# Splitting a query tile: two casts in a row and one subtraction on 128 rows

## The chip, the cores and the metric

One core of a Trainium2 chip runs the kernel. The metric is the device time of one execution in microseconds (us). TensorE (PE; its weight loads are PEld) multiplies, VectorE (DVE), ScalarE (ACT) and GpSimd (POOL) work on tiles, and SyncE (SP) issues nearly all transfers. Each engine runs its own queue in order and waits on semaphores.

## The reference

One decoder layer on x of 2048 x 1024 in float32. Cut to what matters here:

```python
h = rmsnorm(x, norm1)
q, k, v, b_gate, c_gate, hc, p = split(h @ w_in)          # 512 | 128 | 128 | 3 x 256 | 256
scores = einsum('bnqhgd,bnkhd->bnhgqk', qb, k_band) / 8    # 8 query heads of 64, 2 key heads
probs  = softmax over a band of 128 keys, with bias and a sink per head
mixed  = concat([probs @ v_band, short_conv(...), pool(...)])
x = x + mixed @ w_out
x = x + relu(rmsnorm(x, norm2) @ w1)**2 @ w2
out = rmsnorm(x, final_norm)
```

## The kernel before, in words

Matrix products run in TensorE's fp32r format. To keep float32 accuracy each operand is split in two: a high part (ScalarE casts the value to fp32r) and a low part (value minus high part, by VectorE or GpSimd). A product is then three matmuls, high x high, high x low and low x high (lines 285 to 287).

The first part of the kernel, some 620 us, runs over four blocks b of 512 tokens. Channels lie on the 128 rows of a tile, tokens on its columns. In each block 14 column tiles of the input projection are computed in the order `IN_ORDER` (tiles 0 to 3 are queries, 4 keys, 5 values, the others the convolution's and the pool's), each into one of three PSUM banks (`pj`). Eight units of attention, one for each of 128 query rows and each key head, are laid between these projections; then come eight tiles of the output projection (`po`). Block 0 has one peculiarity: its normalisation is applied after the product, so that VectorE writes the product times `rb` to a tile `z` in SBUF, and what follows reads `z`. In blocks 1 to 3 what follows reads the PSUM bank itself. In block 3 VectorE and SP also prepare the MLP's first inputs (`xb`, lines 784 to 830).

For scores, a query tile holds two heads, 64 rows each. `do_q` writes a tile `q` of 128 x 2 x 512: for head a, the high part lies on the head's own 64 rows and the low part on the other 64, so that one matmul against keys stacked in the same way (`Kd`) adds both. The low part is computed on the head's own rows (`ql`), and a transfer on SP carries it to the other 64 rows. The scores (`sc`, lines 610 and 611) of the first unit with these heads need both the cast and the landed transfer.

Weights come through a ring of six raw tiles (`wr`, line 208, on SP's queue), are cast by ScalarE (`wh`, line 263) and completed by GpSimd or VectorE (`wl`, line 264), in a second ring of six.

The order of instructions on each engine is not the order of the code: a scheduler that runs when the program is built places them by estimated times. A change in one function therefore moves instructions elsewhere too. Stores are collected in a list `late` and issued at the next weight step.

Of the kernel before, what the change touches and what calls it, by code (L numbers as in the profile page):

```python
# [12 lines left out]
F32R = mybir.dt.float32r  # L13
I32 = mybir.dt.int32
AF = mybir.ActivationFunctionType
ALU = mybir.AluOpType
# [10 lines left out]
HD = 64  # L27
# [52 lines left out]
def f32(ap):  # L80
    return ap.bitcast(F32)
# [3 lines left out]
def tile_trunk(  # L85
# [14 lines left out]
    pe, act, dve, gp, sp = nc.tensor, nc.scalar, nc.vector, nc.gpsimd, nc.sync  # L100
# [11 lines left out]
    raw_src, plan, late = [], [], []  # L112
# [199 lines left out]
    def tmp(name):  # L312
        return pB.tile([P, T], F32, tag="tmp", name=name, bufs=4)
# [218 lines left out]
    def proj(b, i, mid=None, bank=None):  # L532
        if b == 0 and i in first:
            ps = first[i]
            flush()
        else:
            xh, xl = xhl[b]
            ps = ps_mm.tile([P, T], F32, tag="mm", name=f"pj{b}_{i}") if bank is None else bank
            for k in range(KC):
                if k % HC == 0:  # L540
                    hi, lo = w_next()
                if k == HC and mid:
                    mid()
                latest[0] = mm3(ps, hi[:, k % HC], lo[:, k % HC], xh[:, k], xl[:, k], k == 0, k == KC - 1)
        return ps
# [42 lines left out]
    def do_q(b, i, ps):  # L588
        q = pA.tile([P, 2, T], F32R, tag=f"q{i}", name=f"q{b}_{i}")
        ql = tmp(f"ql{b}_{i}")  # L590
        for a in range(2):
            o = a * 64
            act.copy(q[o : o + 64, a], ps[o : o + 64])
            dve.tensor_tensor(
                out=ql[o : o + 64].bitcast(F32R), in0=ps[o : o + 64], in1=f32(q[o : o + 64, a]), op=ALU.subtract
            )
            z = 64 - o
            late.append(lambda o=o, z=z, a=a: sp.dma_start(f32(q[z : z + 64, a]), ql[o : o + 64]))
        Q[b, i] = q


# [252 lines left out]
    for i in range(4):  # L854
        evac[i] = lambda b, ps, i=i: do_q(b, i, ps)
# [6 lines left out]
    for b in range(NB):  # L862
# [10 lines left out]
        for i in IN_ORDER[:NPRE]:  # L873
            ps = proj(b, i)
# [6 lines left out]
        for n, i in enumerate(IN_ORDER[NPRE:]):  # L881
# [7 lines left out]
            ps = proj(b, i, mid)  # L889
# [329 lines left out]
    kept, ps = {}, {}  # L1219
    for i, (o, q, pp_, cs) in enumerate(steps):  # L1220
# [18 lines left out]
        if q == NQ - 1:  # L1239
# [3 lines left out]
            ps = {}  # L1243
# [98 lines left out]
```

## Time and profile before

| | |
|---|---|
| median of 3 runs | 1916.68 us (1915.47 to 1917.81) |
| the profiled execution | 1912.7 us, span 1910.9 us, mean granted clock 0.992 |
| PE busy | 1875.3 us (98%) |
| DVE, ACT, POOL busy | 1114.4, 894.2, 1020.9 us |
| attention and projections, four blocks | about the first 620 us |

A view by stretches gives busy time of each engine in a window, counted in us from the span's start. A view of waits names the waiting engine and line and what released it. Where a row says `[0.36 <-DMA q<-ql]`, the engine had been idle for 0.36 us and the transfer of ql to q ended that. Line numbers are those of the kernel before; in the changed kernel the lines after 598 have numbers smaller by one.

### The profile page before, as it was taken

To read this page: it belongs to the slowest core of one execution; us is meant where nothing else is said; L and a number is where in the kernel's file an instruction comes from. 1 tells how busy PE (TensorE), PEld (TensorE's weight loads), DVE (VectorE), ACT (ScalarE), POOL (GpSimd) and SP (SyncE) were. 2 spreads that over 40 slices of the span, in tenths; PEclk is the share of its full clock that TensorE was granted. 3 is DMA by queue.
4 is the path that set the end of the run, shared out by engine and by line. 5 is a ranking of instruction groups with operands and counts; after the bars stand their busy time and mean duration, and the time that the engine had idled before them with its cause. 6 is when DMAs were issued, how large, how long until landed. Compare 5 with 4: busy or idle time off the path is not lost.

```text
span 1910.9 us, 25904 instructions
## 1 busy us (share of the span) xinstructions
PE 1875.3 (98%) x8507; PEld 1527.7 (80%) x8507; DVE 1114.4 (58%) x1606; ACT 894.2 (47%) x1637; POOL 1020.9 (53%) x745
## 2 busy tenths in 40 slices
PE   8989999999899999999999999999999999999998
PEld 6867887888787888888878888888888888888887
DVE  5695585576888577865574444442525264533465
ACT  6654664663476444554565455442323222225332
POOL 5667566575563645654464444434666665526520
PEclk9999999999999999999999999999999999999999
DMA  8417426425936779765686656588777666645244
GB/s 261 139 61 219 123 67 208 129 72 183 313 105 217 241 252 316 274 219 195 226 282 202 198 178 194 187 276 281 238 236 237 196 214 203 221 131 166 99 160 138
DMA packets 202938, 375.46 MB, mean 196 GB/s; under 512 B 22775, under 2 KB 43316, under 8 KB 202804
## 3 DMA queue, kind: packets, MB, share of 16 engines
q1 hardware_dynamic: 201992, 373.20, 60.3%
q8 instruction: 67, 1.10, 0.2%
q10 hardware_dynamic: 812, 0.61, 0.1%
q14 instruction: 67, 0.55, 0.1%
HBM read 249.45 MB, written 117.98 MB: 192 GB/s over the span
## 4 chain that ended last, share of the span: by engine, by line
PE 84%; DMA 6%; DVE 6%; issue 2%; ACT 1%; POOL 1%; SPq 1%; DVEq 0%; POOLq 0%; ACTq 0%
PE o L285 11%; PE o L286 11%; PE o L287 11%; PE bT L287 6%; PE bT L286 6%; PE bT L285 6%; PE bB L285 4%; PE bB L286 4%; PE bB L287 4%; PE pj L286 4%; PE pj L285 4%; PE pj L287 4%; PE po L286 1%; PE po L285 1%; PE po L287 1%
## 5 line engine op out<-in xcount | busy, mean ns | idle before, releaser
L264 POOL TENSOR_TENSOR wl<-wr,wh 128x512 fp32r<-128x512 f32 x354 | 502.9, 1427 | 516.0 <-ACT wh L263 477.8
L263 ACT CAST wh<-wr 128x512 fp32r<-128x512 f32 x416 | 254.5, 617 | 345.5 <-PE bT L286 62.6
L784 DVE TENSOR_TENSOR bl<-br,bh 128x1024 fp32r<-128x1024 f32 (+2 forms) x144 | 186.9, 1301 | 320.9 <-ACT bh L1131 318.0
L286 PE MATMUL o<-bl,wh 128*128 128x512 f32 (+1 forms) x960 | 362.0, 380 | 0.0
L287 PE MATMUL o<-bh,wl 128*128 128x512 f32 (+1 forms) x960 | 361.2, 380 | 0.0
L285 PE MATMUL o<-bh,wh 128*128 128x512 f32 (+1 forms) x960 | 349.7, 380 | 0.0
L286 PEld LDWEIGHTS o<-bl,wh 128*128 128x128 f32 x960 | 180.9, 188 | 36.6 <-DVE bl L784 0.2
L287 PEld LDWEIGHTS o<-bh,wl 128*128 128x128 f32 x960 | 180.8, 188 | 36.7
L285 PEld LDWEIGHTS o<-bh,wh 128*128 128x128 f32 x960 | 176.4, 188 | 36.4
L286 PE MATMUL bT<-hlT,wh 128*128 128x512 f32 x512 | 202.2, 395 | 1.0 <-POOL hlT L987 1.0
L287 PE MATMUL bT<-hhT,wl 128*128 128x512 f32 x512 | 202.0, 395 | 0.0
L285 PE MATMUL bT<-hhT,wh 128*128 128x512 f32 x512 | 201.8, 394 | 0.0
L285 PE MATMUL pj<-xh,wh 128*128 128x512 f32 x440 | 177.7, 405 | 7.0 <-ACT wh L263 6.5
L286 PE MATMUL pj<-xl,wh 128*128 128x512 f32 x440 | 176.2, 401 | 4.1 <-DVE xl L419 4.1
L287 PE MATMUL pj<-xh,wl 128*128 128x512 f32 x440 | 176.3, 401 | 0.0
L264 POOL TENSOR_TENSOR wl<-s,wh 128x512 fp32r<-128x512 f32 x64 | 92.2, 1440 | 137.7 <-ACT wh L263 128.9
L263 ACT CAST wh<-s 128x512 fp32r<-128x512 f32 x64 | 39.7, 621 | 247.4 <-PE o L286 238.8
L1131 ACT CAST bh<-br 128x1024 fp32r<-128x1024 f32 (+2 forms) x144 | 123.2, 856 | 64.4 <-PE o L287 55.5
L285 PE MATMUL bB<-hhB,wh 128*128 128x512 f32 x384 | 151.7, 395 | 0.0
L286 PE MATMUL bB<-hlB,wh 128*128 128x512 f32 x384 | 151.4, 394 | 0.0
L287 PE MATMUL bB<-hhB,wl 128*128 128x512 f32 x384 | 151.3, 394 | 0.0
L231 POOL TENSOR_TENSOR s<-wr,wr 128x512 f32<-128x512 f32 x64 | 127.9, 1999 | 15.3 <-DMA wr<-in_w_dram 10.6
(186 smaller groups left out, 3368.5 us busy)
## 6 DMA issues: line engine op xcount, KB each, us to landing
wr<-in_w_dram SPq DMA_DIRECT2D x256, 256.0 KB, 3.6
hop_T<-s SPq DMA_DIRECT2D x128, 256.0 KB, 2.9
wr<-in_win_dram SPq DMA_DIRECT2D x112, 256.0 KB, 4.3
hop_B<-h SPq DMA_DIRECT2D x96, 256.0 KB, 3.3
br<-hop_B SPq DMA_DIRECT2D x48, 512.0 KB, 4.5
br<-hop_T SPq DMA_DIRECT2D x48, 512.0 KB, 4.5
wr<-ss_T SPq DMA_DIRECT2D x48, 256.0 KB, 2.9
wr<-in_wout_dram SPq DMA_DIRECT2D x36, 256.0 KB, 2.6
```

The source lines that it names most:

```text
L231: gp.tensor_tensor(out=t, in0=a, in1=b, op=op)
L263: act.copy(hi, src)
L264: eng.tensor_tensor(out=lo, in0=src, in1=f32(hi), op=ALU.subtract)
L285: pe.matmul(ps, hi, xh, start=first, stop=False)
L286: pe.matmul(ps, hi, xl, start=False, stop=False)
L287: return pe.matmul(ps, lo, xh, start=False, stop=last)
L784: return dve.tensor_tensor(out=out, in0=a, in1=b, op=ALU.subtract)
L1131: mark["act"] = act.copy(hi, src)
```

## The change

ScalarE first casts all 128 rows into the first half of `q` (the rows of head 1 there are scratch, and the transfer of head 0's low part overwrites them), and then the 64 rows of head 1 into the second half. VectorE then subtracts once, on 128 rows. The two transfers are as before, 64 rows each, and both now follow the one subtraction.

```diff
     def do_q(b, i, ps):
         q = pA.tile([P, 2, T], F32R, tag=f"q{i}", name=f"q{b}_{i}")
         ql = tmp(f"ql{b}_{i}")
+
+        act.copy(q[:, 0], ps)
+        act.copy(q[HD:, 1], ps[HD:])
+        dve.tensor_tensor(out=ql.bitcast(F32R), in0=ps, in1=f32(q[:, 0]), op=ALU.subtract)
         for a in range(2):
-            o = a * 64
-            act.copy(q[o : o + 64, a], ps[o : o + 64])
-            dve.tensor_tensor(
-                out=ql[o : o + 64].bitcast(F32R), in0=ps[o : o + 64], in1=f32(q[o : o + 64, a]), op=ALU.subtract
-            )
-            z = 64 - o
-            late.append(lambda o=o, z=z, a=a: sp.dma_start(f32(q[z : z + 64, a]), ql[o : o + 64]))
+            o, z = a * HD, (1 - a) * HD
+            late.append(lambda o=o, z=z, a=a: sp.dma_start(f32(q[z : z + HD, a]), ql[o : o + HD]))
         Q[b, i] = q
```

What the scheduler makes of it is shown at three places. On SP's queue in block 0, where the first query tiles are sent (q_0 and q_1 are the query tiles, ql their low parts, wr a weight load, xr the next block's input, wx a table of weights), before:

```order
L598 DMA q_0_684<-ql_0_685 64x512 x2
L598 DMA q_1_694<-ql_1_695 64x512
L208 DMA wr_782<-in_win_dram 128x512
L377 DMA xr_6_1229<-in_xT_dram 128x512
L598 DMA q_1_694<-ql_1_695 64x512
```

and now:

```order
L597 DMA q_0_684<-ql_0_685 64x512 x2
L208 DMA wr_780<-in_win_dram 128x512
L597 DMA q_1_693<-ql_1_694 64x512 x2
L377 DMA xr_6_1225<-in_xT_dram 128x512
L377 DMA xr_7_1313<-in_xT_dram 128x512
```

q_1's first transfer moved behind a weight load, its second ahead of an input load.

On VectorE in block 3, between the first unit's scores and the second's (s and nm are a unit's scores and their maximum, rd the reciprocal of the denominator, xb the MLP's inputs), before:

```order
L627 RECIPROCAL rd_0_0_5298<-den_0_0_5297 128x4
L784 TENSOR_TENSOR xb_2_5617<-xb_2_5617,xb_3_5618 128x512
L784 TENSOR_TENSOR xb_1_5833<-xb_3_5835,xb_1_5833 128x512
L594 TENSOR_TENSOR ql_3_5471<-pj_3_5404,q_3_5470 64x512
L628 TENSOR_TENSOR s_0_0_5294<-s_0_0_5294,rd_0_0_5298 128x4x256
L594 TENSOR_TENSOR ql_3_5471<-pj_3_5404,q_3_5470 64x512
L620 ISA s_1_0_5385,nm_1_0_5387<-sc_1_0_5376,bias,nsink 128x256
```

and now:

```order
L626 RECIPROCAL rd_0_0_5284<-den_0_0_5283 128x4
L783 TENSOR_TENSOR xb_2_5601<-xb_2_5601,xb_3_5602 128x512
L783 TENSOR_TENSOR xb_1_5817<-xb_3_5819,xb_1_5817 128x512
L627 TENSOR_TENSOR s_0_0_5280<-s_0_0_5280,rd_0_0_5284 128x4x256
L594 TENSOR_TENSOR ql_3_5456<-pj_3_5389,q_3_5455 128x512
L619 ISA s_1_0_5370,nm_1_0_5372<-sc_1_0_5361,bias,nsink 128x256
```

One subtraction is gone and the other stands behind the normalisation of s.

On TensorE in block 0, where the scores of the second unit (1,0) stand among the projection's matmuls (pj_12 and pj_13 are column tiles 12 and 13), before:

```order
L287 MATMUL pj_12_922<-xh_362,wl_761 128x512
L285 MATMUL pj_13_1026<-xh_362,wh_778 128x512
L286 MATMUL pj_13_1026<-xl_363,wh_778 128x512
L287 MATMUL pj_13_1026<-xh_362,wl_779 128x512
L285 MATMUL pj_13_1026<-xh_362,wh_778 128x512
L610 MATMUL sc_1_0_804<-Kd,q_0_684 128x256
```

and now:

```order
L285 MATMUL pj_12_918<-xh_362,wh_758 128x512
L286 MATMUL pj_12_918<-xl_363,wh_758 128x512
L287 MATMUL pj_12_918<-xh_362,wl_759 128x512
L285 MATMUL pj_12_918<-xh_362,wh_758 128x512
L286 MATMUL pj_12_918<-xl_363,wh_758 128x512
L609 MATMUL sc_1_0_801<-Kd,q_0_684 128x256
```

The scores moved ahead of the last matmul of tile 12 and of the first four of tile 13.

## The prediction

> **What bounds the kernel now.** I read the page's head and chain first, then a table by stretches, then TensorE's waits, then the tile that the change touches.
>
> ```profile
> span 1910.9 us, 25904 instructions
> PE 1875.3 (98%) x8507; PEld 1527.7 (80%) x8507; DVE 1114.4 (58%) x1606; ACT 894.2 (47%) x1637; POOL 1020.9 (53%) x745
> ...
> PE 84%; DMA 6%; DVE 6%; issue 2%; ACT 1%; POOL 1%; SPq 1%; DVEq 0%; POOLq 0%; ACTq 0%
> ```
>
> TensorE works 1875.3 of 1910.9 us and makes up 84% of the chain that ended last. Its idle time is 35.6 us in all, and no change to casts and subtractions can win more than a part of that and of what low clocks add to it. So I ask where TensorE is idle while the touched blocks run. In the table by stretches the first number is the stretch's length; then PE, PEld, DVE, ACT and POOL busy time, granted clock, DMA share and GB/s:
>
> ```profile
> 115.00:180.00 65.00, 59.66 (x250) 46.91 (x249) 47.09 (x68) 31.71 (x61) 37.70 (x29) 0.95 0.47 144
> 180.00:250.00 70.00, 69.21 (x351) 57.34 (x350) 42.23 (x106) 45.76 (x110) 44.95 (x40) 1.00 0.48 133
> 500.00:580.00 80.00, 76.66 (x392) 63.20 (x391) 69.14 (x146) 50.70 (x127) 47.44 (x39) 1.00 0.53 176
> 620.00:1200.00 580.00, 579.02 (x2486) 469.01 (x2485) 353.98 (x455) 296.95 (x503) 298.29 (x208) 1.00 0.68 231
> ...
> 60.00:95.00 35.00, 35.00 (x189) 29.76 (x188) 23.50 (x63) 24.47 (x68) 26.76 (x26) 1.00 0.31 87
> 95.00:130.00 35.00, 32.45 (x153) 25.75 (x152) 34.21 (x62) 21.34 (x51) 25.36 (x22) 0.95 0.22 68
> ...
> 135.00:140.00 5.00, 3.91 (x10) 2.86 (x11) 4.44 (x7) 3.72 (x7) 2.31 (x2) 0.70 0.00 0
> ```
>
> Block 1's attention (180 to 250) leaves 0.8 us idle. The end of block 0 (115 to 180) leaves 5.3 us and block 3's attention (500 to 580) 3.3 us; there VectorE is the busy one (34.2 of 35 us from 95 to 130, 69.1 of 80 from 500 to 580). From 620 to 1200 TensorE idles 1.0 us of 580, at 579.02/2486 = 0.233 us per matmul, so time won earlier is kept. After a stall the granted clock is lower for some microseconds (0.70 from 135 to 140), so a stall costs more than its idle time. TensorE's waits by cause (total, times, longest):
>
> ```profile
> PE sc L610 <- DMA q<-ql: 3.4, 5, 1.5
> PE po L285 <- ACT mxh L688: 2.3, 1, 2.3
> PE av L649 <- DVE ao L658: 1.8, 2, 1.7
> PE pt L638 <- DVE s L628: 0.9, 1, 0.9
> PE sc L610 <- DVE nm L620: 0.8, 1, 0.8
> PE po L286 <- POOL mxl L689: 0.7, 1, 0.7
> PE av L650 <- DVE ptl L642: 0.6, 1, 0.6
> ```
>
> Only the first row, 3.4 us, is a wait for a q tile itself, and it is for the transfer, not for the split.
>
> **The change part by part.** What an instruction costs stands in the rows of the tiles (minimum, median, maximum in ns) and in the groups by form:
>
> ```profile
> L593 ACT CAST q<-pj x24: 575/581/584, 189.9 to 528.2; 64x512 fp32r<-64x512 f32 x24
> L594 DVE TENSOR_TENSOR ql<-pj,q x24: 672/688/695, 190.5 to 529.4; 64x512 fp32r<-64x512 f32 x24
> L594 DVE TENSOR_TENSOR ql<-z,q x8: 672/687/1369, 44.3 to 60.7; 64x512 fp32r<-64x512 f32 x8
> ...
> L642 DVE TENSOR_TENSOR ptl<-pt,pth x62: 673/689/693, 67.9 to 589.0; 128x512 fp32r<-128x512 f32 x62
> ...
> L641 ACT CAST pth<-pt 128x512 fp32r<-128x512 f32 x62 | 34.7, 587 | 4.0 <-PE pt L638 3.2
> ```
>
> A 128-row subtraction from PSUM takes 689 ns where a 64-row one takes 688, and a 128-row cast 587 where a 64-row one takes 581. So VectorE goes from 32 subtractions to 16, 16 x 0.688 = 11.0 us less work, and ScalarE keeps 32 casts, 16 of them 128 rows, 0.1 us more. Neither engine sets the span; 11.0 us is an upper bound that only a VectorE-bound stretch could pass on.
>
> The order of waits changes too. Before, in blocks 1 to 3, the second cast waits for the first subtraction and the second subtraction for the second cast (total, times, longest):
>
> ```profile
> ACT q L593 <- DVE ql L594: 14.0, 10, 4.9
> DVE ql L594 <- ACT q L593: 9.1, 9, 2.5
> ```
>
> After, the two casts stand next to each other on ScalarE. I take it that the subtraction follows both, since before no two engines read one PSUM tile at once, not even its two halves (the waits just shown). The 14.0 us of ScalarE's queue held up by VectorE go. ScalarE is idle half the time and no wait of TensorE's above ends on it through these casts, so I price that at nothing: the cover is the ring of six split weight tiles.
>
> *Block 0 (43 to 60 us).* The tile comes from SBUF, so the subtraction needs the first cast only. On SP's queue the first transfer of q_1 now stands behind a weight load:
>
> ```profile
> 46.88 3.66 SPq L598 DMA_DIRECT2D q<-ql  x3
> 50.64 0.53 SPq L208 DMA_DIRECT2D wr<-in_win_dram  x1
> ...
> 52.68 0.48 SPq L598 DMA_DIRECT2D q<-ql  x1
> ...
> 55.32 0.33 PE L610 MATMUL sc<-Kd,q 128*128 128x128 f32 x1 [0.96 <-DMA q<-ql]
> ...
> 56.06 0.33 PE L610 MATMUL sc<-Kd,q 128*128 128x128 f32 x1 [0.30 <-DMA q<-ql]
> ```
>
> The third issue of the first row is q_1's head 0; it gets 0.53 plus about 0.1 us later. Head 1 (52.68) leaves about 1.0 us sooner. q_0's issues, for which TensorE waits 0.96 us at 55.32, follow the wx store as before and do not move. The low end is that block 0's waits go (this one and 0.30 at 56.06, together 1.3 us), the high end that q_1's head 0 adds 0.65 and its transfer as much again behind the load's: +1.2. I take +0.5, since q_1's scores come right behind q_0's.
>
> *Blocks 1 and 2.* The chain for q_1 of block 1, with what TensorE waits for:
>
> ```profile
> 195.45 0.58 ACT L593 CAST q<-pj 64x512 fp32r<-64x512 f32 x1
> 196.07 0.68 DVE L594 TENSOR_TENSOR ql<-pj,q 64x512 fp32r<-64x512 f32 x1
> 196.78 0.58 ACT L593 CAST q<-pj 64x512 fp32r<-64x512 f32 x1 [0.75 <-DVE ql L594]
> 197.45 0.69 DVE L594 TENSOR_TENSOR ql<-pj,q 64x512 fp32r<-64x512 f32 x1
> 196.78 0.47 SPq L598 DMA_DIRECT2D q<-ql  x1
> 198.25 0.47 SPq L598 DMA_DIRECT2D q<-ql  x1
> 203.01 0.36 PE L610 MATMUL sc<-Kd,q 128*128 128x256 f32 x1 [0.36 <-DMA q<-ql]
> ```
>
> Now: 195.45 + 0.58 + 0.58 + about 0.1 of handover + 0.69 = 197.4 for both heads, against 196.75 for head 0 and 198.1 for head 1. Head 0 is 0.65 us late, head 1 is issued 0.5 behind it at about 198.0, 0.2 us early. The wait of 0.36 us is for head 0, so it can grow. The bounds for both blocks are -0.6 (both blocks' waits go: 3.4 less 1.3 and less 1.5 in block 3) and +1.3 (0.65 in each); I take +0.3, for the new order also puts the scores of q_1 behind more projection matmuls there.
>
> The Trainium skill, "PSUM — Partial Sum Buffer", section Terms, says that two engines may not touch the same bank and 32-partition quadrant at once, reads included, while different quadrants of one bank may be used together. By that rule the old wait between the two halves was not forced by the chip, and the new subtraction, which shares rows 64 to 127 with the second cast, must come after it: the rule speaks against this change by just the 0.65 us of head 0. If the subtraction needed the first cast alone, this term would be -0.6 and the sum 0.9 lower; no row of before shows the new form.
>
> *Block 3.* VectorE and SP are late here, not the casts:
>
> ```profile
> 499.78 0.68 DVE L594 TENSOR_TENSOR ql<-pj,q 64x512 fp32r<-64x512 f32 x1
> ...
> 503.62 0.49 SPq L598 DMA_DIRECT2D q<-ql  x1
> ...
> 527.53 0.67 DVE L594 TENSOR_TENSOR ql<-pj,q 64x512 fp32r<-64x512 f32 x1
> ...
> 529.37 0.69 DVE L594 TENSOR_TENSOR ql<-pj,q 64x512 fp32r<-64x512 f32 x1
> ```
>
> q_0's head 0 is subtracted by 500.46 but issued only at 503.62, behind stores and loads that stay where they are. The longest score wait (1.5 us) is for it, and stays: 0, between -1.5 and +0.65. Later the waits for s (0.9) and nm (0.8) lie in a stretch where VectorE does not pause; one subtraction of q_2 is gone ahead of them and q_3's now stands behind s. That brings VectorE forward by 2 x 0.69 = 1.4 us by the second wait. The two waits together lose 1.4 of their 1.7: -1.4, between -1.8 and 0.
>
> *End of block 0.* From 95 to 130 VectorE is the limit; from 60 to 95 it idles 11.5 us waiting on TensorE. The new order reaches the scores of unit (1,0) five matmuls sooner, 5 x 0.233 = 1.2 us, so VectorE can start its backlog sooner. If all of it comes through, the stalls between 120 and 135 end 1.2 us earlier; the low end adds the lower clock behind them (-3), the high end is that it goes the other way (+3). I take -1.0.
>
> **The sum.** +0.5 + 0.3 + 0 - 1.4 - 1.0 = -1.6 us. The profiled execution took 1912.7 us (span 1910.9 and 1.8 around it), which gives 1911.1; it lies 4.0 us under the median of the runs, 1916.68. On that median the forecast is 1915.1 us. A measurement here can tell about 0.2%, 3.8 us.
>
> **The rivals.** *A: the VectorE-bound stretches open up.* If the end of block 0 loses half its waits (2.3 + 1.7 + 0.7 + 0.6 = 5.3 us) and the slow clock behind them (1.5 us at 135 to 140 and as much at 120 to 130), that is -4.2; with block 3's -1.8 the time is 1910.7. For it: VectorE is at 34.2 of 35 us. Against: none of the removed subtractions lies between 95 and 130. *B: the transfers come late (slower).* If the 0.65 us of head 0 and a load's issue of 0.53 fall on the first scores of all four blocks, 4 x 1.2 = +4.8 with nothing won: 1921.5. It decides from 3.8 us, that is when more than three blocks wait in full; the waits of 0.36 us show the slack is near nothing in block 1, but block 3 is held by SP. *C: the scores come too soon (slower).* TensorE's queue is in order; attention 1.2 us earlier in each block makes it wait for VectorE, 4 x 1.2 = 4.8, and the clock after such stalls adds about half as much (1.5 us lost at 0.70 from 135 to 140, after about 3.1 us of idle time): +7.2, less block 3's 1.4: +5.8, 1922.5. It decides from three blocks on. Block 1 has VectorE time to spare (42.2 of 70 us), which speaks against it.
>
> **How the numbers follow.** Forecast 0.55, A 0.27, B 0.09, C 0.09. The forecast's own range is 1913.0 to 1919.0. The range over the cases is 1909.0 to 1920.0: it takes in A's value and stops short of B and C at their full price. Faster by over 0.2%: 0.27; within: 0.55; slower: 0.18.
>
> **What would show it.** Right: 16 subtractions ql at about 690 ns, no wait of a cast q for ql, VectorE near 1103 us busy; waits of sc for q near 4 us; s and nm gone from TensorE's waits near 530; the stretch 115 to 180 about as idle as now. Wrong: that stretch under 3 us or over 8 us idle, new waits of sc over 1 us in blocks 1 and 2, or a 128-row subtraction well over 0.7 us.

## The result, and the profile after

The changed kernel takes 1919.4 us (median; 1916.2 to 1925.6), the kernel before 1915.0 us on the same occasion. The ratio is 1.0028, with a 95% interval of 1.0020 to 1.0035: slower by 0.28%, about 5 us. The time lies inside the range of the prediction, but not in its main case (1913.0 to 1919.0), which was no difference with a sum of -1.6 us, and it moved the other way. That the range holds it is luck: its high end was set by two rivals, and not by what happened.

The page of the profiled execution, its head and the chain that ended last:

```profile
span 1914.4 us, 25845 instructions
...
PE 1875.4 (98%) x8507; PEld 1526.8 (80%) x8507; DVE 1112.7 (58%) x1590; ACT 894.0 (47%) x1637; POOL 1015.1 (53%) x745
...
PE 81%; DVE 8%; DMA 6%; issue 2%; ACT 1%; SPq 1%; POOL 0%; DVEq 0%; ACTq 0%; POOLq 0%
```

TensorE works as long as before (1875.4 us against 1875.3). VectorE has 16 instructions less, yet is only 1.7 us less busy (1112.7 against 1114.4), where 1103 was expected. That is the first thing to explain. VectorE's share of the chain rose from 6 to 8%.

The split itself became what the prediction said it would. The rows of the tile ql (minimum, median, maximum in ns), and then, among the waits (total, times, longest), that of the subtraction for a cast:

```profile
L594 DVE TENSOR_TENSOR ql<-pj,q x12: 676/692/693, 193.0 to 534.7; 128x512 fp32r<-128x512 f32 x12
L594 DVE TENSOR_TENSOR ql<-z,q x4: 676/686/1299, 44.4 to 61.8; 128x512 fp32r<-128x512 f32 x4
```

```profile
DVE ql L594 <- ACT q L593: 10.3, 6, 3.1
```

16 subtractions, about 0.69 us each but for one of 1.30 in block 0; ScalarE no longer waits for VectorE here (14.0 us before), and the subtraction waits for the second cast, line 593, as assumed. So VectorE does save its 11 us on ql. They were spent elsewhere. VectorE's groups by form (busy time and mean ns of one behind the bar), the multiplication that normalises s, before and after:

```profile
L628 DVE TENSOR_TENSOR s<-s,rd 128x1024 f32<-128x1024 f32 x30 | 40.2, 1341 | 0.9
```

```profile
L627 DVE TENSOR_TENSOR s<-s,rd 128x1024 f32<-128x1024 f32 x30 | 51.5, 1718 | 1.0
```

The same 30 instructions, which nobody touched, take 11.3 us more. TensorE's waits over the whole execution, and by the stretches of the prediction:

```profile
PE pj L286 <- DVE xl L419: 6.8, 6, 2.9
...
PE sc L609 <- DMA q<-ql: 3.5, 4, 1.9
...
PE po L285 <- ACT mxh L687: 2.4, 1, 2.4
...
PE pt L637 <- DVE s L627: 2.2, 3, 1.0
PE av L648 <- DVE ao L657: 2.2, 3, 0.9
PE po L285 <- ACT mxh L729: 2.0, 1, 2.0
```

```profile
115.00:180.00 65.00, 59.25 (x252) 46.00 (x251) 45.06 (x63) 30.20 (x58) 39.38 (x31) 0.97 0.47 146
180.00:250.00 70.00, 67.99 (x344) 56.38 (x344) 42.16 (x99) 44.09 (x107) 41.73 (x38) 1.00 0.48 134
```

The wait for the q tiles is 3.5 us (3.4 before), the end of block 0 idles 5.75 us (5.3 before). New are waits for s and for ao. Two of each lie in blocks 1 and 2, the middle blocks, where there was none before. The stretch of block 2, from 347 to 447:

```profile
PE av L648 <- DVE ao L657: 0.6, 1, 0.6
PE pt L637 <- DVE s L627: 0.6, 1, 0.6
PE sc L609 <- DMA q<-ql: 0.6, 1, 0.6
```

Where the time is lost shows in the rows of the eight small matmuls pst_n, which stand early in each block and again in its output projection. Block 2 before and after:

```profile
343.94 0.95 PE L327 MATMUL pst_n<-ones,acc 128*128 128x1 f32 x8
442.14 0.95 PE L327 MATMUL pst_n<-ones,acc 128*128 128x1 f32 x8
```

```profile
346.67 0.95 PE L327 MATMUL pst_n<-ones,acc 128*128 128x1 f32 x8
447.21 0.95 PE L327 MATMUL pst_n<-ones,acc 128*128 128x1 f32 x8
```

98.2 us before, 100.5 after. The other distances between these rows in the two traces: the start of block 1 (49.6 us before) is 1.9 us longer, the rest of block 1 (98.8) 0.6, the start of block 2 (50.4) 0.3, and block 3 behind its row at 498.42 (168.4) is 1.7 us shorter. The 1.9 us are a wait for xl, which is taken up under block 0 in the part on the prediction. Why one multiplication takes 2 us and not 1.2 can be seen where VectorE, GpSimd and TensorE are read side by side. Block 1 of the changed kernel, timeline of the three engines:

```profile
260.63 1.28 POOL L699 TENSOR_TENSOR ps<-ps 64x512 f32<-64x512 f32 x1
...
260.68 2.31 DVE L627 TENSOR_TENSOR s<-s,rd 128x1024 f32<-128x1024 f32 x1
263.02 0.69 DVE L657 TENSOR_TENSOR ao<-av,ao 64x512 f32<-64x512 f32 x1
...
263.13 0.41 PE L637 MATMUL pt<-ident,s 128*128 128x128 f32 x2 [0.65 <-DVE s L627]
```

GpSimd started 0.05 us ahead and ran to 261.91; the multiplication ended at 262.99, 1.08 us behind that, and TensorE waited for it. Where the multiplication comes first, it is GpSimd that takes longer. The kernel before:

```profile
238.04 1.22 DVE L628 TENSOR_TENSOR s<-s,rd 128x1024 f32<-128x1024 f32 x1
...
238.47 1.95 POOL L264 TENSOR_TENSOR wl<-wr,wh 128x512 fp32r<-128x512 f32 x1 [0.38 <-ACT wh L263]
```

1.22 us for the multiplication, and 1.95 for a split of a weight tile (wl), which takes 1.30 in the median. Over both traces the 60 multiplications on 128x1024 follow one rule. In 35 of them no GpSimd instruction with 0.15 us or more to go was running when they started: all took 1.21 to 1.23 us. The other 25 took 1.39 to 3.35 us. Before, 8 of 30 start behind GpSimd; after, 17 of 30. The worst one, again in block 1 of the changed kernel, lost twice:

```profile
238.41 1.30 POOL L662 TENSOR_TENSOR mxl<-ao,mxh 64x512 fp32r<-64x512 f32 x1
...
238.84 3.35 DVE L627 TENSOR_TENSOR s<-s,rd 128x1024 f32<-128x1024 f32 x1
...
239.81 1.29 POOL L264 TENSOR_TENSOR wl<-wr,wh 128x512 fp32r<-128x512 f32 x1
```

It started while mxl ran, and ended 1.09 us behind wl, which started a whole microsecond later than the multiplication.

### The profile page after: what moved, and what is told of

It is laid out like the page before. It is cut to its first block, busy times and chain, and to the rows that moved or that the text cites. A ratio compares the mean times of both kernels' runs of the same rounds, so it can differ in the third digit from the quotient of the medians.

```text
span 1914.4 us, 25845 instructions
## 1 busy us (share of the span) xinstructions
PE 1875.4 (98%) x8507; PEld 1526.8 (80%) x8507; DVE 1112.7 (58%) x1590; ACT 894.0 (47%) x1637; POOL 1015.1 (53%) x745
## 4 chain that ended last, share of the span: by engine, by line
PE 81%; DVE 8%; DMA 6%; issue 2%; ACT 1%; SPq 1%; POOL 0%; DVEq 0%; ACTq 0%; POOLq 0%
PE o L285 11%; PE o L286 11%; PE o L287 11%; PE bT L287 6%; PE bT L286 6%; PE bT L285 6%; PE bB L285 4%; PE bB L287 4%; PE bB L286 4%; PE pj L286 3%; PE pj L287 3%; PE pj L285 3%; DVE xl L419 1%; PE po L286 1%; PE po L287 1%
## 5 line engine op out<-in xcount | busy, mean ns | idle before, releaser
L264 POOL TENSOR_TENSOR wl<-wr,wh 128x512 fp32r<-128x512 f32 x354 | 497.6, 1411 | 521.6 <-ACT wh L263 470.7
```

Of the source, the lines that this page charges most:

```text
L264: eng.tensor_tensor(out=lo, in0=src, in1=f32(hi), op=ALU.subtract)
```

## The experiments

Each was timed beside the kernel before. Rows of experiments have line numbers larger by 20 to 30 behind `do_q`. In the code cuts `...` and words in brackets stand for what is not shown. Three theories: *collision* (the scheduler's new order starts the multiplication behind GpSimd), *order* (the new order is bad for TensorE in itself), and *split* (the subtraction after both casts sends head 0's low part late). First, the change in one block at a time.

```diff
-        (old split in all blocks)
+        new split if b == 0 (1, 2, 3) else old split
```

> The new split in block 0 alone; blocks 1 to 3 split as before. Both theories name where the changed kernel's loss arises. Order theory (the scheduler's new order makes VectorE, GpSimd and SP meet differently; the split itself costs nothing): block 0 itself stays within 0.3 us, and SP's queue is late by about 1.2 us behind the first stores of the output projection, so that TensorE waits for xl at the start of block 1 as in the changed kernel (about 2.0 us in all, 0.3 before): +1.5 to +2 us. Split theory (head 0's low part leaves 0.65 us later and the scores wait for it): the waits of sc for q in 45 to 75 grow from 1.3 to over 2 us, +1 us or more, and no wait for xl.

> The new split in block 1 alone. Order theory: the eight multiplications s<-s,rd of block 1 go from 10.2 us in all to about 14.9 us, because GpSimd runs an instruction when they start; TensorE gets new waits for s and ao of about 1.2 us between 255 and 280, and block 1 ends 0.6 us later; total +0.5 to +1. No new wait for xl at the start of block 1. Split theory: waits of sc for q at about 205 grow to 1 us, the multiplications stay at 1.23 us, total +0.7 to +1.3.

> The new split in block 2 alone. Order theory: the same as in block 1 but with less slack ahead of it: multiplications s<-s,rd from 10.2 to about 14.9 us, new waits of pt for s (0.6) and av for ao (0.6), the first output projection row of block 2 about 2.3 us later; total +2 to +2.5. Split theory: only the wait of sc for q grows (0.2 to 0.6 us), total +0.4.

> The new split in block 3 alone. In the changed kernel the distance from the start of block 3 to its end shrinks by 1.8 us. Both theories that keep the sum of the prediction for this block expect a gain: the wait of sc for nm (0.8 us) goes and that of po for xo falls from 3.6 to 2.5; total -1.4 to -1.9 us. If the gain were only the shadow of the delay before it (work on the other queues catching up while block 3 starts later), the total is 0 to +0.5.

| new split in | median us | ratio (interval) | the 8 multiplications of that block, us |
|---|---|---|---|
| block 0 | 1914.3 | 1.0000 (0.9991 to 1.0010) | 12.0 (10.7 before) |
| block 1 | 1919.0 | 1.0021 (1.0011 to 1.0032) | 14.9 (10.2 before) |
| block 2 | 1916.3 | 1.0013 (1.0004 to 1.0023) | 14.9 (10.2 before) |
| block 3 | 1912.9 | 0.9994 (0.9984 to 1.0004) | 11.9 (11.1 before) |

The last column is summed from the rows of the timeline. The four ratios multiply to 1.0028, the whole. The loss is in blocks 1 and 2. For block 0 both theories expected +1 us or more; none came. For block 1 they expected 0.5 to 1.3 us, and it cost 4: in its trace the block itself is 1.6 us longer (100.4 us between its rows, 98.8 before), and the rest lies in block 3 and behind, where nothing was edited, so that part stays unexplained. Block 3 goes the expected way, though its interval holds 1.

Then four tests of the mechanism. In e5 and e6 the multiplication reads one tensor from SBUF and a scalar for each row, the first head's denominator; the other three are left out:

```diff
-        dve.tensor_tensor(out=s[...], in0=s[...], in1=rd.unsqueeze(2).to_broadcast([P, 4, n]), op=ALU.mult)
+        if b in (1, 2):
+            junk = cst.tile([P, 1], F32, tag="junk", bufs=2)
+            dve.tensor_scalar(out=s[...], in0=s[...], scalar1=rd[:, 0:1], scalar2=1.0,
+                              op0=ALU.mult, op1=ALU.mult, accum_out=junk)
+        else:
+            (the multiplication as before)
```

In e7 the subtraction stands between the casts, in e8 a store changes its queue:

```diff
         act.copy(q[:, 0], ps)
+        dve.tensor_tensor(out=ql.bitcast(F32R), in0=ps, in1=f32(q[:, 0]), op=ALU.subtract)
         act.copy(q[HD:, 1], ps[HD:])
-        dve.tensor_tensor(out=ql.bitcast(F32R), in0=ps, in1=f32(q[:, 0]), op=ALU.subtract)
```

```diff
-            sp.dma_start(row[...], t[:m])
+            (act if a == "n1" else sp).dma_start(row[...], t[:m])
```

> The changed kernel with one edit: in blocks 1 and 2 the multiplication that normalises s (s<-s,rd) is an instruction with one tensor from SBUF and the first head's denominator as a scalar for each row, with a sum beside it, instead of one with two tensors from SBUF (so that three heads of four are divided by the wrong denominator). The order of the instructions in these blocks stays that of the changed kernel but for some 10 moved by one or two places. Collision theory (with two tensors from SBUF it waits until a running GpSimd instruction ends): the eight multiplications of a block fall from 14.9 to about 9.5 us although GpSimd is as busy under them; TensorE's waits for s and ao in blocks 1 and 2 go; 4 to 6 us less than the changed kernel, ratio to before about 1.000. Order theory without collision (attention stands too early among the projections and TensorE waits for VectorE whatever this instruction costs): the waits for s and ao stay above half, ratio 1.002 to 1.003. Split theory (the late head 0): 1.002 to 1.003 and the waits of sc for q unchanged.

> The same edit on the kernel before, to see what it is worth where little collides: the eight multiplications of a block go from 10.2 to about 9.5 us. Collision theory: no difference, ratio 0.999 to 1.001. If the edit itself shortens the path by something else than the collisions, the ratio falls below 0.998, and e5 has to be read against that.

> One subtraction on 128 rows as in the change, but written ahead of the second cast: cast of 128 rows, subtraction of 128 rows, cast of head 1's 64 rows. The scheduler then keeps the old order in blocks 1 and 2 nearly whole (113 of 8421 TensorE instructions moved in the whole program, 427 with the change). Collision and order theories: the multiplications of blocks 1 and 2 stay at about 10.2 us each, VectorE's busy time falls by nearly the whole 11 us to about 1104, no new waits for s and ao; ratio 0.998 to 1.000. Split theory, in its form that one subtraction on 128 rows by itself is the harm: as slow as the changed kernel, 1.002 to 1.003.

> The changed kernel, with the store of the next block's normalisation row (row_n<-row, line 353) issued from ScalarE's queue and not from SP's; nothing else moves. In the changed kernel SP reaches it 1.5 us later at the end of block 0, behind a load of xo that waits for a store of xo. If this lateness is part of the loss, TensorE's wait for xl at the start of block 1 (1.4 and 0.6 us) goes and those ahead of blocks 2 and 3 shrink: 1.5 to 4 us less than the changed kernel, ratio about 1.001. If the late store only shows up behind another limit (VectorE's chain for hf), the wait stays near 2 us, ratio 1.002 to 1.003.

| | median us | ratio (interval) |
|---|---|---|
| e5, change, one-source multiplication | 1896.8 | 0.9907 (0.9892 to 0.9921) |
| e6, old split, one-source multiplication | 1894.9 | 0.9899 (0.9886 to 0.9912) |
| e7, cast, subtraction, cast | 1914.2 | 1.0005 (0.9993 to 1.0017) |
| e8, change, row store from ScalarE | 1915.1 | 1.0008 (0.9998 to 1.0017) |

No theory had expected that e5 and e6 would both be far faster than the kernel before, by 17 and 19 us; that is taken up below. Within e5, VectorE's groups by form show both kinds in one execution:

```profile
L656 DVE TENSOR_TENSOR s<-s,rd 128x1024 f32<-128x1024 f32 x14 | 21.7, 1551 | 0.4
L651 DVE TENSOR_SCALAR_CACHE_REDUCE s<-s,rd 128x1024 f32<-128x1024 f32 x16 | 20.5, 1280 | 0.6
```

All 16 with one tensor from SBUF took 1.28 us, 10 of them started while GpSimd had 0.4 to 1.05 us to go. e5 changes the kind of instruction together with the number of its tensors, but rows of before in which only the place of an input differs agree. The subtraction ptl<-pt,pth reads one tensor from PSUM and one from SBUF; 30 of its 62 started while GpSimd had 0.37 to 1.28 us to go, and none took over 0.693 us. The subtraction ql<-z,q of block 0 reads both from SBUF; the one of 8 that started with 0.82 us to go took 1.369 (the maximum in the prediction's rows). So the delay needs the second tensor from SBUF. The Trainium skill, "SBUF — State Buffer", section Who interferes with whom, states this: a VectorE instruction with both inputs in SBUF contends with GpSimd's reads, and the one that starts second is blocked. The traces agree, with 1.22 us free and 1.39 to 3.35 behind GpSimd, but for the row of 3.35 us, where a GpSimd instruction that started later was not held back. TensorE's waits in blocks 1 (195 to 345) and 2 (345 to 447) of e5:

```profile
PE sc L631 <- DMA q<-ql: 1.2, 3, 0.6
PE pj L286 <- DVE xl L419: 0.6, 1, 0.6
```

```profile
PE sc L631 <- ACT vt L575: 1.5, 1, 1.5
PE sc L631 <- DMA q<-ql: 0.6, 2, 0.4
```

The waits for s and ao are gone with the order of the changed kernel nearly untouched, which speaks against the order theory. What stays is waits of the scores for q. (The row with vt is probably one of them: the scores do not read vt. They started at 352.45; the first query tile's transfers were issued at 344.0 and 344.6, and their landing is not in the trace. Of the transfers beside them one of Kd took 8.2 us to land and one of q 6.8.) In e7 one subtraction on 128 rows shows no harm. VectorE is at 1105.1 us, and the multiplications stay short:

```profile
L649 DVE TENSOR_TENSOR s<-s,rd 128x1024 f32<-128x1024 f32 x30 | 42.5, 1415 | 0.8
```

The ratio holds 1, so 9.3 us less work on VectorE bring no gain that can be told from none either.

Nearly all of the gain lies behind 650 us, where nothing was edited: from the row pst_n near 670 to the end the changed kernel took 1244.0 us and e5 1225.7. The experiments e5 and e6 had added a small tile, which moves the tiles behind it. So:

```diff
+        if b == 1:
+            cst.tile([P, 1], F32, tag="junk", bufs=2)      # never used
```

> The kernel before with nothing changed but an unused tile of 4 bytes a row in two buffers, put where the one-source experiments had theirs: the instructions and their order are the same to the last one, and the tiles that lie behind it in SBUF (among them the split weights wh and wl, which TensorE loads) move by 64 bytes. The two one-source experiments were both 19 us faster, and their traces show it not in the blocks they edit but after 650 us, in the pace of the matmuls (1200 to 1910: 702 us busy before, 687 and 686 in them). Address theory: the shift alone does it, ratio 0.990. Rival (the wrong denominators change what the later blocks compute, or the instruction itself has an effect that lasts): no effect here, ratio 1.000.

> The same unused tile in the changed kernel. If the change costs what it cost without it, this is 0.28% above the kernel before with the tile: about 5 us more than e9, the eight multiplications of blocks 1 and 2 at 14.9 us each again, and TensorE's waits for s and ao back in both blocks (0.6 us each). If the loss itself was a matter of addresses, e9 and e10 take the same time.

> The version that the experiments point to: the unused tile; one subtraction on 128 rows written ahead of the second cast in blocks 0 to 2 (old order nearly kept), the change as it is in block 3 (where it gained), and the store of the normalisation row from ScalarE's queue. If the three add up: 0.990 from the tile, -0.1% from block 3, -0.1 to -0.2% from the row: 0.987 to 0.989. If the parts are within the noise of each other, 0.990.

> The kernel before with the store of the normalisation row on ScalarE's queue, as in e8. The row then no longer stands behind xo's loads on SP's queue. If the lateness of this store is a loss of the changed kernel alone (0.3 us of wait for xl at the start of block 1 before, 2.0 after), the ratio stays at 1.000; if it helps both kernels alike, 0.998 to 0.999, and then e8's gain over the changed kernel is no part of what the change cost.

| | median us (range) | ratio (interval) |
|---|---|---|
| e9, old split, unused tile | 1894.4 (1893.1 to 1895.7) | 0.9896 (0.9883 to 0.9910) |
| e10, change, unused tile | 1901.3 (1900.3 to 1902.8) | 0.9933 (0.9921 to 0.9946) |
| e11, unused tile, e7's split, change in block 3, row store | 1890.5 (1889.2 to 1894.4) | 0.9883 (0.9866 to 0.9901) |
| e12, old split, row store from ScalarE | 1912.2 (1908.5 to 1918.0) | 0.9992 (0.9981 to 1.0002) |

The shift by 64 bytes alone makes the kernel 20 us faster. With it the change costs 6.9 us (e10 less e9), their ranges far apart. TensorE's waits in e10's block 2, with the collisions back:

```profile
PE sc L631 <- DMA q<-ql: 1.5, 3, 0.9
PE sc L631 <- ACT vt L575: 1.3, 1, 1.3
PE pt L661 <- DVE s L651: 0.7, 1, 0.7
PE av L672 <- DVE ao L681: 0.7, 1, 0.7
```

Against this, e5 is 4.5 us less than e10, while the same edit on the old split gave 0.5 us more (e6 less e9). So by the run times the collisions are about 5 of the 6.9 us. The 2 us that stay (e5 less e6) are not clear of the noise: the intervals of the two overlap. By the traces the collisions' part is smaller: in e10's blocks 1 and 2 TensorE waits 2.7 us for s and ao, where e9 has no such wait, and about as much longer than in e9 for q. These runs can say no more than that the collisions are some 3 to 5 us of it. e11 beats both kernels: 1.2% less than before, nearly all of it the shift. Five more runs ask what the rest is.

> e5 (the change, one-source multiplication in blocks 1 and 2, tiles shifted by 64 bytes as there) with the store of the normalisation row on ScalarE's queue. e5 took 1896.8 us, its counterpart with the old split (e6) 1894.9. If the late row is what remains, 1895 us or less; if the low parts' lateness remains, 1896 to 1897 us with the waits of sc for q in blocks 1 and 2 still over 2 us.

> The unused tile, and of the change only the order of the casts: both casts first (64 rows each), then the two subtractions of 64 rows. Head 0's low part leaves about 0.6 us later, VectorE's work is the old one. Against e9 (1894.4 us): if the late low parts cost, waits of sc for q grow in blocks 1 to 3 and the time is 1895.5 to 1897; if not, 1894 to 1895. The multiplications of blocks 1 and 2 stay near 10.2 us each unless the little that moves brings them behind GpSimd.

> The unused tile and e7's form in all blocks: cast of 128 rows, one subtraction on 128 rows, second cast. Nothing leaves later than before, VectorE has 16 subtractions less. Against e9 (1894.4 us): 1892 to 1894.5 if the single subtraction is harmless and the old order nearly kept; 1896 or more if one subtraction on 128 rows is itself part of the loss. Against e11 it tells what the row store and block 3's form add.

> Old split, one-source multiplication in blocks 1 and 2, row store on ScalarE's queue, tiles shifted by 64 bytes. If the row was all that kept e5 above e6, e17 and this one take the same time within 1 us; if late low parts or something else remain, e17 is 2 us above this one.

> The kernel of e13 again, beside e16: as slow as e16 within 1 us if collisions and the row store are the whole loss, 2 us slower if not.

Their edits, beside those shown: e14 casts both halves first, then subtracts twice on 64 rows; e13 and e17 are e5 with e8's row store, e16 is e6 with it, and e15 is e7 with the unused tile.

| | median us (range) | ratio (interval) |
|---|---|---|
| e13, e5 and row store | 1893.2 (1889.9 to 1896.9) | 0.9879 (0.9861 to 0.9897) |
| e14, both casts, two subtractions | 1895.6 (1894.2 to 1900.5) | 0.9892 (0.9876 to 0.9908) |
| e15, cast, subtraction, cast | 1897.3 (1896.5 to 1899.0) | 0.9899 (0.9884 to 0.9914) |
| e16, e6 and row store | 1892.4 (1890.7 to 1894.8) | 0.9883 (0.9867 to 0.9900) |
| e17, e13 again | 1894.9 (1891.5 to 1896.5) | 0.9893 (0.9878 to 0.9908) |

e13 seemed to say that the row store was the rest, but e16 gains from it too, 2.4 us against e6, where e13 and e17 gain 3.6 and 1.9 against e5. e13 and e17 are one kernel, and their ratios (0.9879 and 0.9893) lie on both sides of e16's (0.9883), so that no rest can be told from none here, though e17 has a median 2.5 us above e16's. The row store helps the old kernel by some 2 us (e12 and e16) and the changed one by 2 to 4 (e8, e13 and e17), so it is at most a small part of the change's cost. e14 and e15 stand where e9 does by ratio (0.9896). By median, the measure that their expectations name, both fall where a loss was expected, but on an occasion on which the kernel before was 3 us higher too. Neither the adjacent casts nor the single subtraction shows a loss that can be told from none. The waits of the scores in blocks 1 and 2 together, the row with vt counted, are 2.8 us in the mean of the six traces with the new order (0.6 to 3.8) and 1.0 in those of seven runs with the old one there (0.4 to 2.3). In e14, which sends head 0's low part later but subtracts twice, they are 1.8. The difference of 1.8 us is about what remains by the run times, but in the pair of before and after it is 0.0 (0.6 in both), and no run took it away by itself, so it is argued, not shown.

## Why the prediction was wrong

*The step that failed* is the pricing of VectorE's freed time and of blocks 1 and 2. VectorE was to have "16 x 0.688 = 11.0 us less work", and the term of blocks 1 and 2 held nothing but the scores' wait for q, +0.3 us with bounds of -0.6 and +1.3. Alone they cost 0.21 and 0.13% (e2 and e3), 6.5 us, of which a part of e2's lies outside its block. The subtraction was priced by itself, and all other instructions at their old durations. But the scheduler, given 0.69 us less in each split, moved VectorE and GpSimd against each other. In blocks 1 and 2 the eight multiplications went from 10.2 to 14.9 us each, 9.5 us in both, and with 1.6 us in blocks 0 and 3 that is the 11 us that ate the gain. Part of them is on the path: s feeds the transposes of the next step, and TensorE's four new waits for s and ao in blocks 1 and 2 are 2.5 us in the trace of after. With the tile shift the whole costs 6.9 us, 3 to 5 of it this.

*The waits for q in these blocks* were to be between -0.6 and +1.3. In the means of the traces they grew by 1.8 us, a little past the high end; in the pair of before and after they did not grow. Head 0 of the second tile does leave late: in block 2 its low part is ready 1.95 us behind the row pst_n before and 2.8 us after, 0.9 us later where 0.65 was worked out. That lateness came as worked out; what it cost is not shown.

*Block 0 and its end* (+0.5 and -1.0, sum -0.5): the row pst_n in block 0's output projection stands at 145.10 against 145.23, and the new split there alone gave a ratio of 1.0000, with an interval of about 2 us to both sides. So the sum is not contradicted, but neither term is shown: the scores waited 1.0 us for q in block 0, 1.3 before, and TensorE's idle time up to this row, 13.6 us, is no shorter than before, 13.4. Not foreseen was the longer wait for xl, 6.8 us in all after and 4.1 before, most of the difference at the start of block 1 (2.0 us, 0.3 before), with SP's row store 1.5 us later. With the store on ScalarE's queue 0.4 us are left there (e8). But e10, the same order with the store on SP's queue, has no such wait there, so that this wait is not a fixed part of the change.

*Block 3* (-1.4): alone -0.06%, 1.1 us, with an interval from -3.1 to +0.8 us. The wait of sc for nm (0.8 us before) went as said, that of pt for s did not: 1.2 us where 0.9 stood. TensorE's waits of the run with the change in block 3 alone, from 500 to 640:

```profile
PE sc L631 <- DMA q<-ql: 2.9, 2, 2.1
PE po L285 <- DVE xo L766: 2.6, 1, 2.6
PE pt L659 <- DVE s L649: 1.2, 1, 1.2
```

*The rivals.* A did not come. C named the right waits, TensorE for VectorE in blocks 1 and 2, for the wrong reason: not because the scores come too soon, since without the collisions the same order has no such wait. B, the late transfers, came at 1.8 us at most and not at 4.8. None had the mechanism that decided. It was there to be read before: in the trace of before the multiplication's rows by form have a mean of 1341 ns, while most single rows are 1.22 us. The prediction's own rows show it too, in the maximum of ql<-z,q: 1369 ns, twice its median, beside 695 for ql<-pj,q. A group whose mean lies 10% over its usual row, or whose maximum is far over its median, is one to ask what delays it.

*Of the listed signs*, "VectorE near 1103 us busy" failed at once (1112.7), and pointed to the cause; "new waits of sc over 1 us" did not, since the new waits of that trace were those of pt and av, 0.6 to 0.7 us each.

## What to carry to other kernels

When a scheduler places instructions by estimated times, a saving on one engine moves the others too, and instructions that nobody touched can change their duration. After such a change, compare the groups by form of every engine for mean durations that moved, before looking at waits. Ahead of it, look for VectorE instructions with two tensors in SBUF and ask which GpSimd instruction will run when they start; where it matters, see whether one of the two inputs can be a scalar for each row or can come from PSUM, as in the rows here that were not delayed.

## What was not expected of the hardware

*A waiting VectorE instruction can be overtaken.* At 238.84 the multiplication waited for one GpSimd instruction, and then for another that started 0.97 us after it. In simple cases it took as much longer as GpSimd still had to go, less about 0.14 us (0.63 us to go: 1.71 us; 1.24 to go: 2.32).

*An unused tile is worth 1%.* In these two kernels the pace of TensorE's matmuls depends on where the tiles lie: all ten runs with the tile shift have ratios of 0.988 to 0.993, all others 0.999 or more. The stretches after 650 us by windows, before, and in e9 with the same instructions in the same order and the tiles 64 bytes further on:

```profile
650.00:1200.00 550.00, 549.02 (x2368) 444.96 (x2367) 342.85 (x444) 286.45 (x485) 276.97 (x192) 1.00 0.68 231
```

```profile
650.00:1200.00 550.00, 548.46 (x2396) 448.53 (x2395) 342.27 (x445) 289.00 (x490) 280.36 (x193) 1.00 0.69 231
```

At a granted clock of 1.00 in both, 549.02/2368 = 0.2318 us for a matmul against 548.46/2396 = 0.2289. Between the rows pst_n that stand at 666.86 and 1806.84 before, and at 663.95 and 1788.46 in e9, lie 1140.0 and 1124.5 us for the same work. Which of the moved tiles does it, and what it meets there, was not tried.
